# Sub-layer ends of a two-layer decoder trunk: three chunk pairs block by block, a written order for TensorE there, and the last output in quarters

## The chip, the core and the metric

The kernel runs on one NeuronCore of a Trainium2 chip. The metric is the device time of one execution in microseconds (us); the time of before is the median of three executions.

## What is computed

The reference is a two-layer decoder trunk on 256 tokens of width 1024, in fp32. Cut to what matters here:

```python
for l in range(2):
    ...                                   # modulation vectors sh, sc, g from c
    h = x * (1 + sc_a) + sh_a
    mixed = attention(h @ w_in[l])        # three head groups
    x = layer_norm(DN_ALPHA * x + (1 + g_a) * (mixed @ w_out[l]), ln_g[l, 0], ln_b[l, 0])
    h = x * (1 + sc_m) + sh_m
    f = jnp.square(jax.nn.relu(h @ mlp_w1[l])) @ mlp_w2[l]
    x = layer_norm(DN_ALPHA * x + (1 + g_m) * f, ln_g[l, 1], ln_b[l, 1])
```

So there are four sub-layer ends: a product with `w_out` or `mlp_w2`, a LayerNorm over the 1024 columns, and (but for the last) the modulated input of the next sub-layer, transposed.

## The kernel before

The 256 tokens are two blocks of 128 partitions. Every fp32 product is made of three fp32r products: each weight tile is split into a high part `whi` (ScalarE copies, L179) and a low part `wlo` (VectorE, or GpSimd where named, subtracts, L180), and so are the activations (`hT`, `mx`). The split weights go round ten buffers of 1024 columns (pool `spl`, tag "w"); the raw weights come by DMA from SyncE's queue (L138) into four buffers (`raw`).

`w_out` and `mlp_w2` are taken in chunks of 128 rows, two to a pair (one raw buffer): four pairs for `w_out` (`wo`, L1051 to L1053), sixteen for `mlp_w2` (`m2`, L1116 to L1118). A chunk's work for one block and one half of the 1024 columns is three matmuls of 512 columns (hi·hi, hi·lo, lo·hi); "products" below are such threes. Two accumulators of 512 columns per block collect them in PSUM. All pairs but the last two are done for both blocks as they come. The last two are the end: block 0 first, then block 1, so that block 0's normalization runs under block 1's products. `m1` (L368, L369, L371, L372, L1100 to L1103) makes one pair's input `FT` of `mlp_w2`: a product with `mlp_w1`, Relu, Square, and the split of the result.

`transition` is the end of three of the four sub-layers. For each block: times the gate and the residual, and statistics, on VectorE (`times` L405, `sums` L409, `spread` L412, `stats` L416 to L420, with a power on GpSimd); the scaled rows `P` on VectorE and ScalarE (L427, L425, L426); eight transposes on TensorE (`turn`, L454); scale and shift in PSUM (`modulate`, L463 on VectorE, L461 on ScalarE); the high part of `hT` on ScalarE (`high`, L466) and the low part on VectorE (`low`, L470). Behind that stands `work`, the first products of the next sub-layer, as rows (`v_tile`, L385: 24 matmuls named `mmv` for one block and 256 columns, in the order hT hi·w hi, hT lo·w hi, hT hi·w lo). After the `wo` end, `work` is three tiles for each block (`m1_rows`): `v_tile`, Relu and Square on ScalarE (L1083, L1084), and two transposes (`tp`<-`fr`, L1087), whose result is split (L1091, L1092). After layer 0's MLP it is one `v_tile` of 280 columns and two tiles with a copy (`kr`, L1001) and two transposes (L1004) each. `pool_split` gives a piece of the coming weights to GpSimd. `last_norm` is the end of the last sub-layer: it writes the output, block 0 in columns 0:640 and 640:1024 on GpSimd (L539), block 1 in halves on VectorE (L563, L566), and stores them from SyncE's queue (L535).

The order on each engine comes from a scheduler, except inside `manual_schedule`, where the engines named keep the order of the code: VectorE, ScalarE and GpSimd in `transition`, VectorE and GpSimd in `last_norm`. TensorE is not among them. Between the ends, `filler` puts steps of the modulation vectors' work (16 MB of weights over VectorE) into the loop over the MLP's pairs.

Of the kernel before, what the change touches and what calls it, by code (L numbers as in the profile page):

```python
# [120 lines left out]
def trunk_kernel(ctx: ExitStack, tc: tile.TileContext, a):  # L121
    nc = tc.nc
# [47 lines left out]

    SPARE = dict(P=4, qk=3, mx=4)

    def parts(t, n, eng=None, tag="w"):

        if tag == "w":
            hi, lo = (spl.tile([128, 1024], F32R, name=k, tag="w")[:, :n] for k in ("whi", "wlo"))
        else:
            hi, lo = (att.tile([128, 1024], F32R, name=k, tag=tag, bufs=SPARE[tag])[:, :n] for k in ("whi", "wlo"))
# [294 lines left out]
    def transition(products, accs, G, lnb, rnd, weights, spare, work):  # L473

        N = [Norm(b, accs[b], G, lnb) for b in range(2)]
        H = [MakeH(b, N[b], ROUND[rnd]) for b in range(2)]
# [3 lines left out]
        pool_split = lambda: weights and weights.pop(0)(nc.gpsimd)  # L480
        with tc.manual_schedule(engines={E.DVE, E.Activation, E.Pool}):
            for h in range(2):
                products(0, (h,))
                N[0].half(h)
            N[0].stats()
            pool_split()
            pool_split()
            N[0].scaled()
            for jj in range(2):
                H[0].turn(jj)  # L490
            products(1, (0, 1))
            H[0].modulate(0)
# [36 lines left out]
    def last_norm(products, accs, G, lnb):  # L529
# [4 lines left out]
        def store(n, c0, c1):  # L534
            nc.sync.dma_start(a["out"][0, n.b * 128:(n.b + 1) * 128, c0:c1], x[:, n.b, c0:c1])  # L535

        def on_pool(n, c0, c1):
            for i, op in enumerate((OP.mult, OP.add)):
                nc.gpsimd.tensor_tensor(x[:, n.b, c0:c1], (n.r[:, c0:c1], x[:, n.b, c0:c1])[i], lnb[:, i, c0:c1], op=op)  # L539
            store(n, c0, c1)  # L540

        with tc.manual_schedule(engines={E.DVE, E.Pool}):
            n = N[0]
            for h in range(2):
                products(0, (h,))
                n.half(h)
# [6 lines left out]
            n = N[1]  # L553
            for h in range(2):
                products(1, (h,))
                n.half(h)
            n.stats()
            on_pool(N[0], 640, D)
            cuts = ((0, 512), (512, D))
            for c0, c1 in cuts:  # L560
                s = slice(c0, c1)
                o = n.halves[c0 // 512]
                nc.vector.scalar_tensor_tensor(o, o, n.mv[:, 0:1], lnb[:, 0, s], op0=OP.subtract, op1=OP.mult)  # L563
            for c0, c1 in cuts:
                s = slice(c0, c1)
                nc.vector.scalar_tensor_tensor(x[:, 1, s], n.halves[c0 // 512], n.ve[:, 1:2], lnb[:, 1, s],  # L566
                                               op0=OP.mult, op1=OP.add)
                store(n, c0, c1)

# [353 lines left out]
    for l in range(DEPTH):  # L923
# [119 lines left out]

        def wo(b, c2, hs):
            for k, h in ((k, h) for k in range(2) for h in hs):
                c = 2 * c2 + k
                hi, lo = WO[c]
                mh, ml = MX[c2][:, 0, k, b * 128:(b + 1) * 128], MX[c2][:, 1, k, b * 128:(b + 1) * 128]
                s = slice(h * 512, h * 512 + 512)
                o = accs[b][h]  # L1050
                nc.tensor.matmul(o, mh, hi[:, s], start=c == 0, stop=False)  # L1051
                nc.tensor.matmul(o, mh, lo[:, s], start=False, stop=False)  # L1052
                nc.tensor.matmul(o, ml, hi[:, s], start=False, stop=c == 7)  # L1053

        for c2 in range(2):
            WO.extend(split(rawload(a["w_out"][l, c2]), 2, 1024))
            for b in range(2):
                wo(b, c2, (0, 1))
        for c2 in range(2, 4):
            WO.extend(split(rawload(a["w_out"][l, c2]), 2, 1024))  # L1060

# [43 lines left out]
        def load_w2(g):  # L1105
            W2[g] = split(rawload(a["mlp_w2"][l, g]), 2, 1024)

        def m2(g, b, hs):
            f = FT[g]
            t = slice(b * 128, (b + 1) * 128)  # L1110
            for i, h in ((i, h) for i in range(2) for h in hs):
                o = accs[b][h]
                s = slice(h * 512, h * 512 + 512)
                hi, lo = W2[g][i]
                first, lastk = g == 0 and i == 0, g == NG - 1 and i == 1
                nc.tensor.matmul(o, f[:, 0, i, t], hi[:, s], start=first, stop=False)  # L1116
                nc.tensor.matmul(o, f[:, 0, i, t], lo[:, s], start=False, stop=False)  # L1117
                nc.tensor.matmul(o, f[:, 1, i, t], hi[:, s], start=False, stop=lastk)  # L1118

        before = [p for g in range(EARLY) for p in w1_steps(g)]  # L1120
        end = transition(lambda b, h: [wo(b, c2, h) for c2 in (2, 3)], accs, ROUND[l, 3], lnb, (l, 2), before, SPARES[0],
                         [lambda b, g=g: m1_rows(g, b) for g in range(EARLY)])
# [4 lines left out]
        accs = [[ps.tile([128, 512], F32, name="m2", tag=t) for _ in range(2)] for t in ("acc", "sc")]  # L1127
        for g in range(NG - 2):
            with tc.issue_after(end[0]), tc.issue_after(end[1]):
                if EARLY <= g + 2 < NG:  # L1130
                    m1(g + 2)
                load_w2(g)
            for b in range(2):
                m2(g, b, (0, 1))
# [7 lines left out]
        tail = lambda b, h, m2=m2: [m2(g, b, h) for g in (NG - 2, NG - 1)]  # L1142
        if l < DEPTH - 1:
# [73 lines left out]
```

## Time and profile before

| | us |
|---|---|
| median of three runs (705.74 to 707.02) | 705.89 |
| the profiled execution, its own time | 706.43 |
| its span, first to last instruction | 704.7 |
| what lies around the span | 1.7 |
| TensorE busy in the span | 674.1 (96%) |
| VectorE busy | 492.3 (70%) |
| ScalarE busy | 402.6 (57%) |
| GpSimd busy | 39.1 (6%) |

Busy time is from the profiler's records of one execution; matmuls are pipelined and the end of one is modelled, so that spacing from start to start tells what a matmul costs. The mean granted TensorE clock was 0.991 of full speed.

### The profile page before, as it was taken

The numbers are of one execution on the slowest core, as the hardware profiler recorded it, in microseconds if no ns is written. First come the engines' busy times: TensorE is split into PE (matmuls) and PEld (weight loads), VectorE is DVE, ScalarE is ACT, GpSimd is POOL, SyncE is SP. The second block draws the span as 40 slices with busy tenths as digits, with TensorE's granted clock in tenths as the row PEclk, the third lists the DMA queues.
The fourth block names the chain that finished last, engine by engine and source line by source line (L and its number), as shares of the span: only waits on it lengthen the run. The fifth ranks groups of instructions, "written<-read, shape, count | busy, mean of one in ns | idle before, by whom it ended". The sixth has DMA issues, their size and how long they took to land.

```text
span 704.7 us, 11146 instructions
## 1 busy us (share of the span) xinstructions
PE 674.1 (96%) x4284; PEld 550.9 (78%) x4284; DVE 492.3 (70%) x947; ACT 402.6 (57%) x781; POOL 39.1 (6%) x39
## 2 busy tenths in 40 slices
PE   5998899999999999999998999999999999999994
PEld 4898658458788888888878977867788888888883
DVE  3455965657799879798977976657779855555556
ACT  2345473785665546656555447598474655656550
POOL 0000000000400000000013020000220000000003
PEclk9999999999999999999999999999999999999998
DMA  9998686568459989798873757710538955555501
GB/s 337 350 353 312 224 319 231 169 236 312 162 183 363 346 309 344 283 344 327 326 262 120 282 226 274 272 39 23 183 117 294 373 214 195 212 183 180 180 0 60
DMA packets 29553, 167.68 MB, mean 238 GB/s; under 512 B 3199, under 2 KB 6683, under 8 KB 11964
## 3 DMA queue, kind: packets, MB, share of 16 engines
q1 hardware_dynamic: 29436, 166.94, 65.0%
q8 instruction: 34, 0.56, 0.3%
q14 instruction: 19, 0.16, 0.1%
q0 software_dynamic: 64, 0.02, 0.0%
HBM read 165.87 MB, written 1.08 MB: 237 GB/s over the span
## 4 chain that ended last, share of the span: by engine, by line
PE 89%; DVE 4%; ACT 3%; issue 1%; POOL 1%; DMA 1%; SPq 0%; POOLq 0%; DVEq 0%
PE mm L368 14%; PE m L1116 8%; PE m L1117 8%; PE m L1118 8%; PE mmv L385 7%; PE mm L369 7%; PE s L680 3%; PE tp L648 3%; PE gv L168 3%; PE mm L355 2%; PE mm L357 2%; PE mm L356 2%; PE wo L1051 2%; PE wo L1053 2%; PE acc L696 2%; PE wo L1052 2%
## 5 line engine op out<-in xcount | busy, mean ns | idle before, releaser
L180 DVE TENSOR_TENSOR wlo<-raw,whi 128x1024 fp32r<-128x1024 f32 (+2 forms) x166 | 196.8, 1203 | 56.5 <-ACT whi L179 54.9
L179 ACT ACTIVATE whi<-raw 128x1024 fp32r<-128x1024 f32 (+2 forms) x175 | 179.2, 1041 | 56.8 <-PE wo L1052 17.2
L368 PE MATMUL mm<-hT,whi 128*128 128x512 f32 x416 | 148.3, 398 | 0.0
L369 PE MATMUL mm<-hT,wlo 128*128 128x256 f32 x416 | 117.0, 281 | 0.9 <-DVE wlo L180 0.9
L1116 PE MATMUL m<-whi,mx 128*128 128x512 f32 x256 | 100.1, 391 | 0.0
L1117 PE MATMUL m<-wlo,mx 128*128 128x512 f32 x256 | 100.0, 391 | 0.0
L1118 PE MATMUL m<-whi,mx 128*128 128x512 f32 x256 | 99.5, 390 | 0.0
L368 PEld LDWEIGHTS mm<-hT,whi 128*128 128x128 f32 x416 | 78.2, 188 | 20.3 <-ACT whi L179 0.8
L369 PEld LDWEIGHTS mm<-hT,wlo 128*128 128x128 f32 x416 | 78.5, 189 | 2.5 <-DVE wlo L180 1.6
L234 DVE SCALAR_TENSOR_TENSOR qk<-raw,se,qk 128x1024 f32<-128x1024 f32 x56 | 71.4, 1286 | 2.5 <-DMA raw<-in_ada_dram 1.9
L371 ACT ACTIVATE P<-mm 128x256 f32<-128x256 f32 x52 | 19.7, 378 | 73.0 <-PE mm L369 73.0
L385 PE MATMUL mmv<-whi,hT 128*128 128x256 f32 (+2 forms) x352 | 55.9, 304 | 4.7 <-ACT hT L466 4.7
L1116 PEld LDWEIGHTS m<-whi,mx 128*128 128x128 f32 x256 | 48.1, 188 | 11.2 <-ACT whi L179 0.8
L1118 PEld LDWEIGHTS m<-whi,mx 128*128 128x128 f32 x256 | 48.1, 188 | 10.1
L1117 PEld LDWEIGHTS m<-wlo,mx 128*128 128x128 f32 x256 | 48.0, 188 | 8.9
L385 PEld LDWEIGHTS mmv<-whi,hT 128*128 128x128 f32 x352 | 48.8, 194 | 6.9 <-ACT hT L466 5.9
L636 ACT ACTIVATE P<-P,sxt 128x128 f32<-128x128 f32 (+1 forms) x96 | 42.6, 446 | 17.2 <-DVE sxt L634 17.0
L355 PE MATMUL mm<-hT,whi 128*128 128x256 f32 x128 | 37.4, 292 | 0.0
L357 PE MATMUL mm<-hT,wlo 128*128 128x256 f32 x128 | 37.0, 289 | 0.0
L356 PE MATMUL mm<-hT,whi 128*128 128x256 f32 x128 | 36.8, 287 | 0.0
L634 DVE CUSTOM_DVE_ANT_0 P<-s,bias 128x128 f32<-128x128 f32 (+1 forms) x80 | 25.7, 351 | 14.4 <-PE s L680 12.0
L1103 DVE TENSOR_TENSOR mx<-P,mx 128x512 fp32r<-128x512 f32 x26 | 17.9, 690 | 25.6 <-ACT mx L1102 25.6
(215 smaller groups left out, 1090.4 us busy)
## 6 DMA issues: line engine op xcount, KB each, us to landing
raw<-in_mlp_w_dram SPq DMA_DIRECT2D x64, 1024.0 KB, 6.5
raw<-in_ada_dram SPq DMA_DIRECT2D x32, 1024.0 KB, 5.9
raw<-in_adag_dram SPq DMA_DIRECT2D x16, 1024.0 KB, 6.7
raw<-in_w_in_dram SPq DMA_DIRECT2D x9, 1024.0 KB, 6.1
raw<-in_cmp_w_dram SPq DMA_DIRECT2D x8, 1024.0 KB, 6.8
raw<-in_w_out_dram SPq DMA_DIRECT2D x8, 1024.0 KB, 6.8
w<-in_w_in_dram SPq DMA_DIRECT2D x8, 396.0 KB, 7.2
w<-in_w_in_dram SPq DMA_DIRECT2D x8, 384.0 KB, 6.1
```

Of the source, the lines that this page charges most:

```text
L179: nc.scalar.activation(hi, t, AF.Copy)
L180: (eng or nc.vector).tensor_tensor(lo, t, hi.bitcast(F32), op=OP.subtract)
L234: nc.vector.scalar_tensor_tensor(ac, src, by, ac, op0=OP.mult, op1=OP.add)
L355: nc.tensor.matmul(o[:, i], hi[:, c], hT[:, 0, kc], start=kc == 0, stop=False, skip_group_check=True)
L356: nc.tensor.matmul(o[:, i], hi[:, c], hT[:, 1, kc], start=False, stop=False, skip_group_check=True)
L357: nc.tensor.matmul(o[:, i], lo[:, c], hT[:, 0, kc], start=False, stop=kc == KC - 1, skip_group_check=True)
L368: nc.tensor.matmul(o, hi[:, c], hT[:, :, kc], start=kc == 0, stop=False, skip_group_check=True)
L369: nc.tensor.matmul(o[:, 0], lo[:, c], hT[:, 0, kc], start=False, stop=kc == KC - 1, skip_group_check=True)
L385: nc.tensor.matmul(o, hT[:, x_, kc, t], ws[kc][w_], start=kc == 0 and x_ + w_ == 0, stop=kc == KC - 1 and w_ == 1)
L1116: nc.tensor.matmul(o, f[:, 0, i, t], hi[:, s], start=first, stop=False)
L1117: nc.tensor.matmul(o, f[:, 0, i, t], lo[:, s], start=False, stop=False)
L1118: nc.tensor.matmul(o, f[:, 1, i, t], hi[:, s], start=False, stop=lastk)
```

## The change

Each sub-layer end now takes three pairs block by block instead of two, and the code hands `transition` a list of products. TensorE is added to the engines that keep the order of the code, in `transition` and in `last_norm`, where ScalarE is added too. Block 0's eight transposes stand after seven of block 1's twelve products (`TURN`). Of the three pairs, one is split in pieces of 512 columns into buffers of their own (tag "u2"). In `transition`, `scaled` stands before the first `pool_split`, and the second tile of `work` before block 1's transposes. The last `m1` stands ahead of the end. The loop over the MLP's pairs has one turn less, and two filler steps in two turns of three. In `last_norm` block 1's second half is made in two quarters of 256 columns, and its last 192 columns are finished on ScalarE and GpSimd; block 0's output goes in halves.

```diff
+TURN = 6
...
-    SPARE = dict(P=4, qk=3, mx=4)
+    SPARE = dict(P=4, qk=3, mx=4, u2=11)
...
+            m = 512 if tag == "u2" else 1024
+            hi, lo = (att.tile([128, m], F32R, name=k, tag=tag, bufs=SPARE[tag])[:, :n] for k in ("whi", "wlo"))
...
+    def wide(t, small=False):
+
+        hs = [slice(0, 512), slice(512, 1024)]
+        if small:
+            return [[parts(t[:, i * 1024 + h * 512:i * 1024 + h * 512 + 512], 512, None, "u2") for h in range(2)]
+                    for i in range(2)]
+        return [[(hi[:, s], lo[:, s]) for s in hs] for hi, lo in split(t, 2, 1024)]
...
-        with tc.manual_schedule(engines={E.DVE, E.Activation, E.Pool}):
+        with tc.manual_schedule(engines={E.PE, E.DVE, E.Activation, E.Pool}):
             for h in range(2):
-                products(0, (h,))
+                for p in products(0, (h,)):
+                    p()
                 N[0].half(h)
             N[0].stats()
+            N[0].scaled()
             pool_split()
-            pool_split()
-            N[0].scaled()
-            for jj in range(2):
-                H[0].turn(jj)
-            products(1, (0, 1))
+            for i, p in enumerate(products(1, (0, 1))):
+                p()
+                if i == TURN:
+                    for jj in range(2):
+                        H[0].turn(jj)
...
             N[1].scaled()
+            late.append(work[1](0))
             for jj in range(2):
                 H[1].turn(jj)
-            late.append(work[1](0))
...
-        with tc.manual_schedule(engines={E.DVE, E.Pool}):
+        with tc.manual_schedule(engines={E.PE, E.DVE, E.Activation, E.Pool}):
...
-            on_pool(n, 0, 640)
...
-            on_pool(N[0], 640, D)
...
+                on_pool(n, h * 512, h * 512 + 512)
+            for p in products(1, (0,)):
+                p()
+            m.times(0)
+            m.sums(0)
+            for i in range(2):
+                nc.vector.bn_stats(m.st[:, i], m.halves[0][:, i * 256:i * 256 + 256])
+            for i in (2, 3):
+                for p in products(1, (1,), i % 2 * 256, 256):
+                    p()
+                quarter(m, i)
...
+            nc.scalar.activation(r, c, AF.Identity, bias=m.ve[:, 3:4])
+            nc.gpsimd.tensor_tensor(r, r, lnb[:, 0, 832:], op=OP.mult)
+            nc.scalar.activation(r, r, AF.Copy, scale=m.ve[:, 1:2])
+            nc.gpsimd.tensor_tensor(x[:, 1, 832:], r, lnb[:, 1, 832:], op=OP.add)
+            cuts = ((0, 512, m.halves[0]), (512, 832, m.halves[1][:, :320]))
...
+        for c2 in range(1, 4):
+            WO += wide(rawload(a["w_out"][l, c2]), c2 == 1)
...
-        for g in range(NG - 2):
+        for g in range(NG - 3):
...
-                filler(1 + g % 2)
+                filler(1 + (g % 3 > 0))
         filler(100)
-        for g in (NG - 2, NG - 1):
+        m1(NG - 1)
+        for g in (NG - 3, NG - 2, NG - 1):
             load_w2(g)
```

`quarter(m, i)` is `times`, `sums` and statistics on 256 columns. Three places show how the rows on an engine move; the numbers behind names are the tiles'.

TensorE at layer 0's `wo` end, where the first tile of `work` ends and its transposes stand. Before:

```order
L385 MATMUL mmv_1990<-wlo_1870,hT_89 128x256 x4
L385 MATMUL mmv_2036<-whi_1915,hT_89 128x256 x2
L385 MATMUL mmv_2036<-whi_1873,hT_89 128x256 x4
L385 MATMUL mmv_2036<-whi_1915,hT_89 128x256 x2
L1087 MATMUL tp_2018<-p1_78,fr_2015 128x128 x2
L385 MATMUL mmv_2036<-whi_1915,hT_89 128x256 x2
L385 MATMUL mmv_2036<-wlo_1874,hT_89 128x256 x4
```

Now:

```order
L395 MATMUL mmv_1994<-wlo_1850,hT_89 128x256 x4
L395 MATMUL mmv_1994<-wlo_1854,hT_89 128x256 x4
L1117 MATMUL tp_2022<-p1_78,fr_2019 128x128 x2
L395 MATMUL mmv_2034<-whi_1857,hT_89 128x256 x4
L395 MATMUL mmv_2034<-whi_1915,hT_89 128x256 x4
```

Before, eight matmuls of the second tile stand between a tile's last matmul and its transposes; now none does. The same holds at each tile of `work` there but the last, and in layer 1.

TensorE at layer 1's MLP end, from the last row of the last `m1` on (`mx` with a number is a pair's `FT`, `m2` an accumulator). Before, where this `m1` makes `mx_6590`:

```order
L369 MATMUL mm2_6611<-hT_89,wlo_6587 128x256
L1116 MATMUL m2_5451<-whi_6636,mx_6414 128x512
L1117 MATMUL m2_5451<-wlo_6637,mx_6414 128x512
L1118 MATMUL m2_5451<-whi_6636,mx_6414 128x512
L1116 MATMUL m2_5452<-whi_6636,mx_6414 128x512
L1117 MATMUL m2_5452<-wlo_6637,mx_6414 128x512
```

Now, where it makes `mx_6614`:

```order
L379 MATMUL mm2_6635<-hT_89,wlo_6611 128x256
L1147 MATMUL m2_5475<-whi_6660,mx_6438 128x512
L1148 MATMUL m2_5475<-wlo_6661,mx_6438 128x512
L1149 MATMUL m2_5475<-whi_6660,mx_6438 128x512
L1147 MATMUL m2_5475<-whi_6668,mx_6438 128x512
L1148 MATMUL m2_5475<-wlo_6669,mx_6438 128x512
L1149 MATMUL m2_5475<-whi_6668,mx_6438 128x512
L1147 MATMUL m2_5475<-whi_6678,mx_6526 128x512
```

Before, 24 matmuls with `mx_6414` (four accumulators) and six with another `FT` stand ahead of the first that reads `mx_6590`; now six with `mx_6438` and six with `mx_6526`, all on one accumulator, stand ahead of the first that reads `mx_6614`. Layer 0's MLP end moves in the same way.

VectorE at the end of the program, block 1's second half and the output (`st`, `mv` and `ve` are statistics, `lnb` the norm's gain and bias). Before:

```order
L405 TENSOR_TENSOR m2_5454<-m2_5454,G_5786 128x512
L409 SCALAR_TENSOR_TENSOR m2_5454<-x_101,m2_5454 128x512
L412 BN_STATS st_6689<-m2_5454 128x6
L416 BN_AGGR mv_6765<-st_6689 128x2
L418 TENSOR_SCALAR ve_6767<-mv_6765 128x1
L419 TENSOR_SCALAR ve_6767<-mv_6765 128x1
L563 SCALAR_TENSOR_TENSOR m2_5453<-m2_5453,mv_6765,lnb_5448 128x512
L563 SCALAR_TENSOR_TENSOR m2_5454<-m2_5454,mv_6765,lnb_5448 128x512
L566 SCALAR_TENSOR_TENSOR x_101<-m2_5453,ve_6767,lnb_5448 128x512
L566 SCALAR_TENSOR_TENSOR x_101<-m2_5454,ve_6767,lnb_5448 128x512
```

Now, from the fourth quarter on (the same three rows, for the third quarter, stand just ahead):

```order
L554 TENSOR_TENSOR m2_5478<-m2_5478,G_5722 128x256
L555 SCALAR_TENSOR_TENSOR m2_5478<-x_101,m2_5478 128x256
L556 BN_STATS st4_6698<-m2_5478 128x6
L426 BN_AGGR mv_6823<-st4_6698 128x2
L428 TENSOR_SCALAR ve_6825<-mv_6823 128x1
L429 TENSOR_SCALAR ve_6825<-mv_6823 128x1
L596 SCALAR_TENSOR_TENSOR m2_5477<-m2_5477,mv_6823,lnb_5472 128x512
L596 SCALAR_TENSOR_TENSOR m2_5478<-m2_5478,mv_6823,lnb_5472 128x320
L598 SCALAR_TENSOR_TENSOR x_101<-m2_5477,ve_6825,lnb_5472 128x512
L598 SCALAR_TENSOR_TENSOR x_101<-m2_5478,ve_6825,lnb_5472 128x320
```

The three operations behind the last matmul have shrunk from 512 to 256 columns, and the last pair's second operation from 512 to 320. Both quarters lie in one accumulator, `m2_5478`, and in the built program the first matmul of the last quarter waits for L556 of the quarter before it.

## Rows read from the trace of the kernel before

**Rows 1.** Page, part 1: busy time of each engine, share of the span, instructions.

```profile
PE 674.1 (96%) x4284; PEld 550.9 (78%) x4284; DVE 492.3 (70%) x947; ACT 402.6 (57%) x781; POOL 39.1 (6%) x39
```

**Rows 2.** Waits of TensorE by releaser: us in all, number, longest.

```profile
PE mmv L385 <- ACT hT L466: 4.7, 3, 2.2
```

**Rows 3.** Two windows: length; PE, PEld, DVE, ACT, POOL busy; clock; DMA share; GB/s.

```profile
204.00:360.00 156.00, 155.54 (x794) 129.07 (x793) 132.09 (x146) 90.44 (x130) 0.00 (x0) 1.00 0.88 323
375.00:376.00 1.00, 1.00 (x7) 1.00 (x6) 1.00 (x2) 0.00 (x0) 1.00 (x1) 0.50 0.00 0
```

**Rows 4.** Timeline of TensorE at layer 0's `wo` end: start, length, instructions, [idle<-releaser].

```profile
179.72 0.66 PE L454 MATMUL tp<-p,P 128*128 128x128 f32 x4 [0.38 <-DVE P L427]
180.13 0.47 PE L1053 MATMUL wo<-whi,mx 128*128 128x512 f32 x1
...
183.70 2.89 PE L385 MATMUL mmv<-whi,hT 128*128 128x256 f32 x22 [1.26 <-ACT hT L466]
...
187.38 1.12 PE L385 MATMUL mmv<-whi,hT 128*128 128x256 f32 x8
188.47 0.44 PE L1087 MATMUL tp<-p,fr 128*128 128x128 f32 x2
...
196.34 0.40 PE L1087 MATMUL tp<-p,fr 128*128 128x128 f32 x2
```

**Rows 5.** The same stretch on ScalarE.

```profile
187.59 0.38 ACT L1083 ACTIVATE fr<-mmv 128x256 f32<-128x256 f32 x1 [2.51 <-PE mmv L385]
188.00 0.42 ACT L1084 ACTIVATE fr<-fr 128x256 f32<-128x256 f32 x1
...
191.36 1.82 ACT L461 ACTIVATE tp<-tp,sb 128x128 f32<-128x128 f32 x4 [0.20 <-PE tp L454]
...
194.85 1.10 ACT L179 ACTIVATE whi<-raw 128x1024 fp32r<-128x1024 f32 x1
```

**Rows 6.** The same stretch on VectorE.

```profile
182.10 0.69 DVE L405 TENSOR_TENSOR wo<-wo,G 128x512 f32<-128x512 f32 x1
...
184.88 0.68 DVE L470 TENSOR_TENSOR hT<-tp,hT 128x512 fp32r<-128x512 f32 x1
```

**Rows 7.** Timeline of TensorE at layer 0's MLP end.

```profile
373.00 4.05 PE L385 MATMUL mmv<-whi,hT 128*128 128x280 f32 x21 [2.19 <-ACT hT L466]
376.85 1.61 PE L385 MATMUL mmv<-wlo,hT 128*128 128x280 f32 x8
378.29 1.48 PE L385 MATMUL mmv<-whi,hT 128*128 128x256 f32 x11
...
387.13 1.19 PE L385 MATMUL mmv<-wlo,hT 128*128 128x280 f32 x8
388.16 2.06 PE L385 MATMUL mmv<-whi,hT 128*128 128x256 f32 x16
```

**Rows 8.** Timeline from the last `m1` on: its last matmul and the split of its result.

```profile
678.17 0.28 PE L369 MATMUL mm<-hT,wlo 128*128 128x256 f32 x1
...
679.34 0.36 ACT L371 ACTIVATE P<-mm 128x256 f32<-128x256 f32 x1
...
680.61 0.41 DVE L372 TENSOR_TENSOR P<-P,mm 128x256 f32<-128x256 f32 x1
...
681.05 0.63 ACT L1100 ACTIVATE P<-P 128x512 f32<-128x512 f32 x1 [1.35 <-DVE P L372]
...
683.05 0.69 DVE L1103 TENSOR_TENSOR mx<-P,mx 128x512 fp32r<-128x512 f32 x1 [2.02 <-ACT mx L1102]
```

**Rows 9.** Timeline of the program's end: last matmul, VectorE behind it.

```profile
694.40 0.39 PE L1118 MATMUL m<-whi,mx 128*128 128x512 f32 x1
...
694.83 0.70 DVE L405 TENSOR_TENSOR m<-m,G 128x512 f32<-128x512 f32 x1 [0.56 <-PE m L1118]
...
698.72 1.40 DVE L566 SCALAR_TENSOR_TENSOR x<-m,ve,lnb 128x512 f32<-128x512 f32 x2
```

More of the change, by code (lines that the diff above doesn't have):

```diff
@@ L535, in store, with quarter @@
             nc.sync.dma_start(a["out"][0, n.b * 128:(n.b + 1) * 128, c0:c1], x[:, n.b, c0:c1])
+        def quarter(n, i):
+            s = slice(i * 256, i * 256 + 256)
+            h, t = n.halves[i // 2], slice(i % 2 * 256, i % 2 * 256 + 256)
+            nc.vector.tensor_tensor(h[:, t], h[:, t], n.G[:, s], op=OP.mult)
+            nc.vector.scalar_tensor_tensor(h[:, t], x[:, n.b, s], RT2, h[:, t], op0=OP.mult, op1=OP.add)
+            nc.vector.bn_stats(n.st[:, i], h[:, t])
         def on_pool(n, c0, c1):
@@ L540, in on_pool @@
             store(n, c0, c1)
-        with tc.manual_schedule(engines={E.DVE, E.Pool}):
-            n = N[0]
+        n, m = N
+        m.st = sm.tile([128, 4, 6], F32, name="st4", bufs=1)
+        with tc.manual_schedule(engines={E.PE, E.DVE, E.Activation, E.Pool}):
             for h in range(2):
-                products(0, (h,))
+                for p in products(0, (h,)):
+                    p()
                 n.half(h)
@@ L1042, in trunk_kernel, with wo @@
         WO = []
[L1044 to L1060, printed above, removed]
+        def wo(b, c, h):
+            c2, k = divmod(c, 2)
+            hi, lo = WO[c][h]
+            mh, ml = MX[c2][:, 0, k, b * 128:(b + 1) * 128], MX[c2][:, 1, k, b * 128:(b + 1) * 128]
+            o = accs[b][h]
+            nc.tensor.matmul(o, mh, hi, start=c == 0, stop=False)
+            nc.tensor.matmul(o, mh, lo, start=False, stop=False)
+            nc.tensor.matmul(o, ml, hi, start=False, stop=c == 7)
+        WO += wide(rawload(a["w_out"][l, 0]))
+        for b in range(2):
+            for c, h in ((c, h) for c in range(2) for h in range(2)):
+                wo(b, c, h)
+        for c2 in range(1, 4):
+            WO += wide(rawload(a["w_out"][l, c2]), c2 == 1)
         NG = FF // 256
@@ L1105, in load_w2, with m2 @@
         def load_w2(g):
-            W2[g] = split(rawload(a["mlp_w2"][l, g]), 2, 1024)
-        def m2(g, b, hs):
+            W2[g] = wide(rawload(a["mlp_w2"][l, g]), g == NG - 3)
+        def m2(g, i, b, h, c0=0, n=512, l=l):
             f = FT[g]
             t = slice(b * 128, (b + 1) * 128)
[L1111 to L1118, printed above, removed]
+            s = slice(c0, c0 + n)
+            o = accs[b][h][:, s]
+            hi, lo = (w[:, s] for w in W2[g][i][h])
+            first, lastk = g == 0 and i == 0, g == NG - 1 and i == 1
+            late = dict(skip_group_check=l == DEPTH - 1 and g > NG - 4)
+            lastk = lastk or l == DEPTH - 1 and g == NG - 4 and i == 1
+            nc.tensor.matmul(o, f[:, 0, i, t], hi, start=first, stop=False, **late)
+            nc.tensor.matmul(o, f[:, 0, i, t], lo, start=False, stop=False, **late)
+            nc.tensor.matmul(o, f[:, 1, i, t], hi, start=False, stop=lastk, **late)
         before = [p for g in range(EARLY) for p in w1_steps(g)]
-        end = transition(lambda b, h: [wo(b, c2, h) for c2 in (2, 3)], accs, ROUND[l, 3], lnb, (l, 2), before, SPARES[0],
+        end = transition(lambda b, hs: [lambda c=c, h=h: wo(b, c, h) for c in range(2, 8) for h in hs], accs,
+                         ROUND[l, 3], lnb, (l, 2), before, SPARES[0],
                          [lambda b, g=g: m1_rows(g, b) for g in range(EARLY)])
@@ L1133, in trunk_kernel @@
             for b in range(2):
-                m2(g, b, (0, 1))
+                for i, h in ((i, h) for i in range(2) for h in range(2)):
+                    m2(g, i, b, h)
             with tc.issue_after(end[1]):
```

29 lines of the change are left out of this document (12 added, 17 removed).

## Prediction, made before the changed kernel was run

> **What bounds the kernel now.** I read the busy times first: TensorE is busy for 674.1 of 704.7 us [rows 1], so the change can win only TensorE's idle time, its waste at half clock and the tail, and loses what it adds to these. The list of waits shows what stands at the sub-layer ends: three waits for the high part of `hT` on ScalarE, 4.7 in all [rows 2]. The reader is to see there the first matmul of the next sub-layer waiting at each end, 1.26 at layer 0's `wo` end (and about as long in layer 1) and 2.19 at layer 0's MLP end [rows 4, 7]. A smaller one, 0.38, is at the first transposes [rows 4]. Between the ends the window 204 to 360 shows TensorE idle for 156.00 - 155.54 = 0.46 [rows 3]: what is moved within that stretch can win nothing. At the end of the program nothing covers VectorE: from the last matmul's start at 694.40 it has six operations of 512 columns and some small ones, 694.83 to 700.12 [rows 9]. So I looked at each place where the change fixes TensorE's order, for what it must now wait for with nothing else to do.
>
> **The `wo` ends, twice.** *Removed:* the products of the third pair lie between block 0's statistics and its transposes (seven products of three), and five products, 15 matmuls, behind the transposes. A matmul of 512 columns takes (694.40 - 678.17 - 0.11)/71 = 0.227 [rows 8, 9], for 72 of them lie between those two starts, so 15 are 3.4. Before, seven matmuls of the products (1.6) stood among and behind the transposes from 179.72 on, and the wait of 1.26 came after them [rows 4]: 2.9 to cover. I take both waits as gone: 0.38 + 1.26 = -1.64.
>
> *Added, transposes of `work`:* each tile's two transposes read `fr`, which ScalarE makes from the whole tile by Relu (0.38) and Square (0.42) [rows 5]. In the row for 187.38 the first tile is over and eight matmuls of the second run; the transposes start at 188.47 [rows 4], 0.05 after Square's end at 188.42. So the eight matmuls exactly cover the chain, 188.47 - 187.38 = 1.09. In the new order nothing stands between tile and transposes for five of the six tiles, and the built program makes the transposes wait for that Square. Four such waits are 4.36. The third tile's wait is longer: its Relu stands on ScalarE behind block 1's shift and high part, and a weight split of 1.10 comes between Relu and Square [rows 5]. ScalarE's chain from 191.36 to the transposes at 196.34 [rows 4, 5] is 4.98; it begins 0.2 after block 1's transposes; TensorE has only that one tile meanwhile, 24 matmuls of (187.38 - 183.70)/30 = 0.123, 2.95 [rows 4]. So 4.98 + 0.2 - 2.95 = 2.2 (below: 1.09, were ScalarE free).
>
> *Added, the low part:* the first tile now keeps its own order, and its 13th matmul needs the second low part. That ended at 184.88 + 0.68 = 185.56, and 183.70 + 12 x 0.123 = 185.18 [rows 4, 6]: 0.4 late, and 1.1 if one operation of 0.69 more stands ahead on VectorE, as `times` does. I take 0.7 (0 to 1.1). Before, the scheduler had other matmuls there.
>
> One end: 4.36 + 2.2 + 0.7 - 1.64 = +5.6; two: **+11.2**. Queued behind each wait is the whole of TensorE; VectorE and ScalarE hold nothing that another engine could use in that time.
>
> **Layer 0's MLP end.** Removed: the wait of 2.19, and what followed it. In 375 to 376 the granted clock is 0.50 of full speed, the lower of the two levels (1.2 GHz), while it is 1.00 from 204 to 360 [rows 3]. The 29 matmuls of 280 columns from 373.00 to 378.29 took 5.29; eight of them at 387.13 took 1.03, 0.129 each [rows 7], so 29 at full clock are 3.74: 1.55 lost. Behind the waits of 1.26 the matmuls ran at 0.123, at once [rows 4]: no loss. Added: the low part, 0.7, and two of the `kr` tiles' transposes behind their copy, with one ScalarE operation where `work` has two: 1.09 - 0.42 = 0.67 each. -2.19 - 1.55 + 0.7 + 1.34 = **-1.7**.
>
> On this row the Trainium skill has a rule that speaks against the change ("TensorE: Matmul & The Clock Gate", section "HAM oscillation — how this bites in real kernels"): matmuls in bursts with waits between them let the clock fall, and each burst begins at the lower level. The trace agrees after the wait of 2.19 and not after that of 1.26. By the rule the 2.2 waits at both `wo` ends would cost as much again; that is the first rival.
>
> **The last `m1` directly ahead of the end.** Its `FT` passes Relu and a copy, three ScalarE steps and a subtraction: 0.36 + 0.41 + 3 x 0.63 + 0.69 = 3.35, with handovers 3.7 [rows 8]. As it ran, it took 678.28 to 683.74, 5.5, with weight splits in between. Before, 30 matmuls (6.8) covered it; now 12 (2.7) do. Wait: 3.7 - 2.7 = 1.0 in layer 1 where the split stands behind; in layer 0 a chunk of the next layer's weights is split on the same engines, 1.10 more [rows 5], 2.1. Sum **+3.1** (below 0.6, if the chain of layer 0 is as free and handovers are quicker; above 2.8 + 3.9 = 6.7, as it ran).
>
> **Weights of the third pair.** The third pair's split parts are needed 18 matmuls, 4.1, earlier than in a loop over both blocks. Four new splits of half width cost no more than the two they replace, and ScalarE is idle for 302.1 of 704.7 us [rows 1], but in layer 0 VectorE is busy 132.09 of 156 ahead of the end [rows 3]. I take **+0.7**, a third of two splits of 1.10 (0 to 2.2).
>
> **Filler steps.** As many in all, two turns of three with two. In the window VectorE has 24 us free and TensorE 0.46 idle [rows 3]: **0**, covered by the four raw buffers; if a turn overran, a split of 1.10 (0 to 2).
>
> **The tail.** The first 256-column matmul of the last quarter waits for three VectorE operations on the quarter before (same accumulator). An operation of 256 columns takes 0.41 [rows 8], so 3 x 0.41 with handovers is 1.35, plus some 0.3 for the last matmul to drain: +1.65. 36 matmuls of 0.123 in place of 18 of 0.227: 4.43 - 4.09 = +0.3. Behind the last matmul three operations shrink from 0.70 to 0.41, -0.9, and two of the last four from 512 to 320 columns of 0.70 x 320/512, -0.5 [rows 9]. The 192 columns on ScalarE and GpSimd (two of 0.36 and two of about 39.1/39 = 1.0 [rows 1]: 2.7) lie beside VectorE's 2.3 and may end 0.4 later. Sum: 1.65 + 0.3 - 1.4 = **+0.5** (-0.5 to 1).
>
> **Sum.** 11.2 - 1.7 + 3.1 + 0.7 + 0.5 = +13.8. The profiled execution took 706.43 (span 704.7 and 1.7 around it), 0.54 over the median of 705.89, so I take that off: 706.43 + 13.8 - 0.54 = **719.7**.
>
> **Rivals.**
> *The clock falls after the 2.2 waits.* For: the row at half clock after 2.19. Against: the wait comes after a tile at full speed and lies in a dense stretch. Price as there, 1.55 at each of two ends: 722.8.
>
> *TensorE is not held by the waiting transposes* (the other side). If matmuls behind them ran meanwhile, the waits of 13.1 (twice 4.36 + 2.2), the `kr` ones of 1.3 and the 3.1 for `FT` would vanish: 719.7 - 17.5 = 702.2. It decides from the point at which these 17.5 shrink by 13.8, to under a fifth. Against: at 179.72 TensorE waited 0.38 for the transposes' input and the `wo` matmul that stood behind came only at 180.13 [rows 4], though its own inputs were old.
> The Trainium skill says the same ("TensorE: Matmul & The Clock Gate", section "Step-by-step: what each phase is for"): only weight loads are pulled ahead, "The MATMULs themselves stay in program order". By it this rival gives nothing; the row agrees.
>
> *More waiting.* `FT` as it ran (+3.6) and two splits late (+1.5): 724.8. For: VectorE is at 85% ahead of layer 0's end. Against: in layer 1 it has no filler.
>
> *Less waiting.* The third tile 1.09 (-2.2), the low part in time at three ends (-2.1), `FT` 0.6 (-2.5), weights in time (-0.7): 712.2.
>
> *It changes nothing:* were the built order the same, 705.9; but the order shown above differs at each place.
>
> **How the numbers follow.** Forecast 0.56 with its own range 715.5 to 721.5 (half of each bound above); clock 0.18; more waiting 0.10; less waiting 0.09; other side 0.05; nothing 0.02. The predicted time is the forecast's, 719.7. The range 712 to 726 takes in all but the other side, no change and the outer halves of the two waiting rivals: about 0.84. A measurement of this kernel tells about 0.2% (1.4 us): faster 0.05, same 0.02, slower 0.93.
>
> **What would show it.** Right: among TensorE's waits eight for `fr` of about 1.1 and two of 2 or more; no 1.26 or 2.19 for `hT`, but waits of under a us for its low part; a wait for `mx` in each layer before the 13th matmul of an MLP end; one wait of 1.65 for VectorE ahead of the last 18 matmuls; full clock at layer 0's MLP end. TensorE's busy time stays at about 674. Wrong: transposes that start behind a tile without idle time, or idle time between 204 and 360 that the filler's new pace makes. I would be wrong most if ScalarE's chain overlapped the tile's own last matmuls, which no row here shows.

## The result, and the profile after

The changed kernel takes **724.68 us** (median of 4 runs, 722.83 to 726.17) against 705.83 (4 runs): ratio 1.0259, interval 1.0244 to 1.0273, 18.9 us slower. Forecast were 719.7, with 712 to 726. The profiled execution, 722.83 with a span of 721.1, is the quickest of the four, so 16.4 of the 18.9 can be read in its trace; the other 2.5 are the profiled executions' distances to their medians, +1.85 after and -0.60 before.

Part 1 of the page of after:

```profile
PE 677.2 (94%) x4302; PEld 550.3 (76%) x4302; DVE 491.7 (68%) x959; ACT 403.4 (56%) x791; POOL 39.9 (6%) x41
```

TensorE does the same work (3.1 busy us more, against [rows 1]) in a span 16.4 longer: the loss is waiting. TensorE's waits in after, by releaser (us in all, number, longest):

```profile
PE tp L1117 <- ACT fr L1114: 11.6, 10, 2.1
...
PE m L1147 <- ACT mx L1132: 1.9, 2, 1.4
...
PE m L1147 <- DVE st L556: 1.5, 1, 1.5
PE mmv L395 <- DVE hT L480: 1.3, 3, 0.5
PE wo L1082 <- DVE wlo L182: 1.3, 3, 0.8
PE tp L1036 <- ACT kr L1033: 1.1, 2, 0.6
PE sw L824 <- ACT ct L1051: 0.8, 1, 0.8
PE acc L805 <- ACT pT L682: 0.8, 1, 0.8
...
PE tp L680 <- DVE P L674: 0.5, 1, 0.5
```

None of these rows is in the list of before. The 4.7 for the high part of `hT` [rows 2] is gone, and ten waits of the transposes for `fr` stand in its place. TensorE at layer 0's `wo` end, where [rows 4] showed no wait for `fr`:

```profile
182.98 1.60 PE L395 MATMUL mmv<-whi,hT 128*128 128x256 f32 x12
185.04 0.74 PE L395 MATMUL mmv<-whi,hT 128*128 128x256 f32 x4 [0.46 <-DVE hT L480]
185.61 1.11 PE L395 MATMUL mmv<-wlo,hT 128*128 128x256 f32 x8
187.64 0.44 PE L1117 MATMUL tp<-p,fr 128*128 128x128 f32 x2 [0.92 <-ACT fr L1114]
187.84 2.15 PE L395 MATMUL mmv<-whi,hT 128*128 128x256 f32 x16
...
194.90 1.12 PE L395 MATMUL mmv<-wlo,hT 128*128 128x256 f32 x8
198.15 0.44 PE L1117 MATMUL tp<-p,fr 128*128 128x128 f32 x2 [2.13 <-ACT fr L1114]
```

One tile can be followed here: twelve matmuls, a wait for the second low part, the last twelve, and then TensorE stands until Square is done. ScalarE behind the third tile:

```profile
193.20 1.83 ACT L471 ACTIVATE tp<-tp,sb 128x128 f32<-128x128 f32 x4 [1.40 <-PE tp L464]
...
196.43 0.41 ACT L1113 ACTIVATE fr<-mmv 128x256 f32<-128x256 f32 x1
196.70 1.09 ACT L181 ACTIVATE whi<-raw 128x1024 fp32r<-128x1024 f32 x1
197.64 0.45 ACT L1114 ACTIVATE fr<-fr 128x256 f32<-128x256 f32 x1
```

The weight split of 1.09 stands between Relu and Square, as before the change [rows 5]. There the wait had other matmuls beside it; here all of TensorE waits for it.

**Where the 16.4 came from.** I lined up the two traces by the start of the k-th matmul of a group (`wo` or `m`) in a layer. An offset is after minus before; the last column is what was added since the row above.

| matmul | before | after | offset | added |
|---|---|---|---|---|
| layer 0, first `wo` | 156.04 | 156.31 | +0.27 | 0.27 (start of the program) |
| its 61st `wo` | 172.60 | 173.89 | +1.29 | 1.02 (late weights of the third pair) |
| its 49th `m` | 226.98 | 232.36 | +5.38 | 4.09 (`wo` end) |
| its 361st `m` | 364.07 | 371.52 | +7.45 | 2.07 (`FT` late) |
| layer 1, first `wo` | 475.79 | 483.69 | +7.90 | 0.45 (MLP end and attention) |
| its 37th `wo` | 495.49 | 505.95 | +10.46 | 2.56 (first products) |
| its 49th `m` | 555.34 | 569.80 | +14.46 | 4.00 (`wo` end) |
| its 361st `m` | 689.19 | 704.68 | +15.49 | 1.03 (`FT` late) |
| its last `m` | 694.40 | 711.94 | +17.54 | 2.05 (quarters) |
| end of the span | 704.7 | 721.1 | +16.4 | -1.14 (behind the last matmul) |

The last two rows' places in the trace of after, TensorE and then VectorE:

```profile
708.07 0.28 PE L1149 MATMUL m<-whi,mx 128*128 128x256 f32 x1
709.81 0.39 PE L1147 MATMUL m<-whi,mx 128*128 128x256 f32 x1 [1.46 <-DVE st L556]
...
709.32 0.43 DVE L556 BATCH_NORM_STATS2 st<-m 128x6 f32<-128x256 f32 x1
712.26 0.43 DVE L554 TENSOR_TENSOR m<-m,G 128x256 f32<-128x256 f32 x1 [2.50 <-PE m L1149]
...
715.20 1.20 DVE L598 SCALAR_TENSOR_TENSOR x<-m,ve,lnb 128x512 f32<-128x512 f32 x2
```

The two quarters, which should overlap, run one after the other: TensorE waits 1.46 for VectorE, then VectorE 2.50 for TensorE. Against [rows 9] the part behind the last matmul is shorter by the 1.14 of the table.

### The profile page after: what moved, and what is told of

Its sections match the earlier page's. It is cut to its first block, busy times and chain, and to the rows that moved or that the text cites. A ratio compares the mean times of both kernels' runs of the same rounds, so it can differ in the third digit from the quotient of the medians.

```text
span 721.1 us, 11205 instructions
## 1 busy us (share of the span) xinstructions
PE 677.2 (94%) x4302; PEld 550.3 (76%) x4302; DVE 491.7 (68%) x959; ACT 403.4 (56%) x791; POOL 39.9 (6%) x41
## 3 DMA queue, kind: packets, MB, share of 16 engines
HBM read 165.87 MB, written 1.08 MB: 232 GB/s over the span
## 4 chain that ended last, share of the span: by engine, by line
PE 81%; ACT 7%; DVE 7%; DMA 2%; issue 2%; POOL 0%; SPq 0%; POOLq 0%; DVEq 0%; ACTq 0%
PE mm L378 13%; PE m L1147 8%; PE m L1149 8%; PE m L1148 8%; PE mm L379 7%; PE mmv L395 6%; PE s L712 3%; PE gv L169 3%; PE tp L680 2%; DVE wlo L182 2%; PE acc L728 2%; ACT whi L181 2%; PE mm L341 2%; PE wo L1082 2%; PE wo L1081 2%
## 5 line engine op out<-in xcount | busy, mean ns | idle before, releaser
L182 DVE TENSOR_TENSOR wlo<-raw,whi 128x1024 fp32r<-128x1024 f32 (+3 forms) x174 | 196.9, 1155 | 52.9 <-ACT whi L181 51.7
L181 ACT ACTIVATE whi<-raw 128x1024 fp32r<-128x1024 f32 (+3 forms) x183 | 178.5, 1002 | 53.7 <-PE mm L378 17.3
L1147 PE MATMUL m<-whi,mx 128*128 128x512 f32 (+1 forms) x262 | 101.7, 388 | 3.3 <-ACT mx L1132 1.9
L1148 PE MATMUL m<-wlo,mx 128*128 128x512 f32 (+1 forms) x262 | 101.0, 386 | 0.0
L1149 PE MATMUL m<-whi,mx 128*128 128x512 f32 (+1 forms) x262 | 100.8, 386 | 0.0
L1147 PEld LDWEIGHTS m<-whi,mx 128*128 128x128 f32 x262 | 49.2, 188 | 14.8 <-ACT mx L1132 2.7
L1149 PEld LDWEIGHTS m<-whi,mx 128*128 128x128 f32 x262 | 49.2, 188 | 10.8 <-DVE mx L1133 0.9
L395 PE MATMUL mmv<-whi,hT 128*128 128x256 f32 (+2 forms) x352 | 53.0, 299 | 1.3 <-DVE hT L480 1.3
L395 PEld LDWEIGHTS mmv<-whi,hT 128*128 128x128 f32 x352 | 47.3, 189 | 2.6 <-DVE hT L480 1.9
```

The source lines that it names most:

```text
L395: nc.tensor.matmul(o, hT[:, x_, kc, t], ws[kc][w_], start=kc == 0 and x_ + w_ == 0, stop=kc == KC - 1 and w_ == 1)
L1147: nc.tensor.matmul(o, f[:, 0, i, t], hi, start=first, stop=False, **late)
L1148: nc.tensor.matmul(o, f[:, 0, i, t], lo, start=False, stop=False, **late)
L1149: nc.tensor.matmul(o, f[:, 1, i, t], hi, start=False, stop=lastk, **late)
```

## The experiments

In each, the time beside it of before is 705.92 to 706.21 on the same chip. The offsets quoted are against the trace of before, at the matmuls of the table.

**1. TensorE's order free again in the three ends.**

```diff
-        with tc.manual_schedule(engines={E.PE, E.DVE, E.Activation, E.Pool}):
+        with tc.manual_schedule(engines={E.DVE, E.Activation, E.Pool}):
             for h in range(2):
```

> The changed kernel, but TensorE's order is left to the scheduler again in the three ends before the last (three pairs, the buffers, the last m1's place and the end of the output as changed). Theory 'order': the waits of TensorE behind the transposes of fr (11.6 us in the trace of after), of kr (1.1) and for the low part of hT (1.3) go, and of the old 4.7 for the high part some 2 come back: 724.7 - 12 = 713 (709 to 716). Rival 'third pair' (what costs is the third pair itself: late weights, less to do under the attention): 720 or more, with fr's waits gone and others in their place.

702.87, ratio 0.9963 (0.9951 to 0.9976): 21.8 less than the changed kernel, and faster than before. No wait for `fr`, `kr` or the low part is left. The same place of its trace:

```profile
181.71 3.02 PE L395 MATMUL mmv<-whi,hT 128*128 128x256 f32 x23
184.56 1.12 PE L395 MATMUL mmv<-wlo,hT 128*128 128x256 f32 x8
185.52 1.12 PE L395 MATMUL mmv<-whi,hT 128*128 128x256 f32 x8
186.61 0.44 PE L1117 MATMUL tp<-p,fr 128*128 128x128 f32 x2
```

The 23 are the first tile's and some of the second's mixed, which hides the low part, and eight of the second's stand ahead of the transposes. TensorE's written order in the three ends alone turned a change worth -3.0 into one of +18.9. It went beyond the 709 to 716 expected: no wait for the high part of `hT` came back, for which I had allowed 2; the stretch from layer 0's MLP end (361st `m`) to layer 1's first `wo` gained 4.2 (-3.73 in place of +0.45); late weights, `FT` in layer 0 and layer 1's first products cost 1.0, 1.4 and 1.3 less; and the 1.85 between the changed kernel's median and its trace went too.

**2. The order written out, but the transposes behind the next tile.** `m1_rows` and `rows` return their transposes as a function, called one tile later:

```diff
             late.append(work[1](0))
+            late[0] = late[0] and late[0]()
             for jj in range(2):
                 H[1].turn(jj)
+            late[1] = late[1] and late[1]()
...
-            late = [w(1) for w in work]
-            for f in late:
+            turn = work[2](0)
+            for w in work:
+                t = w(1)
+                f = turn and turn()
                 if f:
                     f()
+                turn = t
+            turn()()
```

> The changed kernel with TensorE's order still written out, but each tile's two transposes behind the next tile's 24 matmuls (2.95 us, against a chain of 1.1 and once 5.0 on ScalarE). Theory 'order, and there the place of the transposes': fr's ten waits fall from 11.6 to under 2, kr's to 0, the others stay: 724.7 - 10.5 = 714 (711 to 717). Rival 'a fixed order is dear wherever the rows stand': other waits take their place, 720 or more.

707.43, ratio 1.0026 (1.0015 to 1.0037): 17.3 less. TensorE in its trace at the same place:

```profile
185.71 1.12 PE L395 MATMUL mmv<-wlo,hT 128*128 128x256 f32 x8
186.66 2.06 PE L395 MATMUL mmv<-whi,hT 128*128 128x256 f32 x16
188.56 1.10 PE L395 MATMUL mmv<-wlo,hT 128*128 128x256 f32 x8
189.50 0.38 PE L1125 MATMUL tp<-p,fr 128*128 128x128 f32 x2
189.72 1.09 PE L464 MATMUL tp<-p,P 128*128 128x128 f32 x8
```

A tile of 24 now covers the chain, and no transposes wait for `fr` or `kr`. The `wo` ends fall from +4.09 and +4.00 to -1.84 and -1.86: 5.9 at each, and `fr`'s waits were 11.6 in all. So a fixed order isn't dear wherever the rows stand; the rival falls. It is still 4.6 slower than the free order of experiment 1: by the offsets, 2.0 of this is `FT` in layer 0, 1.0 late weights and 1.3 layer 1's first products. The 17.3 exceed the 10.5 that I expected by three things: the two `wo` ends gave 11.8, where I had under 10; the stretch from layer 0's MLP end to layer 1's first `wo` goes from +0.45 to -3.59, 4.04 where I had 1.1 for `kr`; and the changed kernel's median lies 1.85 over its profiled execution while this one's lies 0.07 over.

**3. Two pairs, with the order written out.** The last `m1` is in the loop with that, as before the change, and no pair goes to the buffers of 512 columns.

```diff
-TURN = 6
+TURN = 3
...
-        for c2 in range(1, 4):
-            WO += wide(rawload(a["w_out"][l, c2]), c2 == 1)
+        for c2 in range(2, 4):
+            WO += wide(rawload(a["w_out"][l, c2]))
...
-        for g in range(NG - 3):
+        for g in range(NG - 2):
...
-        m1(NG - 1)
-        for g in (NG - 3, NG - 2, NG - 1):
+        for g in (NG - 2, NG - 1):
             load_w2(g)
```

> The changed kernel with two pairs done block by block instead of three (as before the change), TensorE's order still written out, no buffers of 512 columns, and block 0's transposes after four of block 1's eight products; the last m1 is then in the loop again. Theory 'order': fr's waits stay at about 11.6; gone are the waits for FT (1.0 and 2.1 by the offsets), for late w_out weights (1.3) and what the attention of layer 1 lost for want of other matmuls (about 2), while the high part of hT may come later by 0.5 at each end: 724.7 - 5.5 = 719 (716 to 722). Rival 'third pair': back to 708 or less.

721.76, ratio 1.0233 (1.0219 to 1.0248), as the theory 'order' has it and 13.8 over the rival's 708. `fr` waits 11.6 again. The offsets say what the third pair and the place of the last `m1` cost together under a written order: from the first `wo` to its 61st 0.00 (was 1.02), at layer 1's first products 0.00 (was 2.56), from the 49th to the 361st `m` +0.11 and 0.00 (were 2.07 and 1.03). In return the transposes of `P` wait three times, 4.5 in all, and the quarters' wait is 2.2. The two `wo` ends add 5.83 and 7.25. They have the same waits of 2.12 for `fr` on the third tile, but the clock fell behind the second of them (at 533.43) and not behind the first (at 198.17):

```profile
197.00:200.00 3.00, 1.83 (x16) 1.83 (x17) 3.00 (x6) 1.50 (x3) 0.00 (x0) 1.00 0.00 0
...
533.00:536.00 3.00, 2.57 (x15) 2.57 (x16) 3.00 (x4) 0.76 (x3) 0.00 (x0) 0.71 0.00 0
```

The rows are windows of 3 us: length; PE, PEld, DVE, ACT, POOL busy; clock; DMA share; GB/s.

**4. The last `m1` a turn earlier.**

```diff
                     m1(g + 2)
+                if g == NG - 4:
+                    m1(NG - 1)
...
         filler(100)
-        m1(NG - 1)
```

> The changed kernel with the last m1 a turn earlier, in the loop, ahead of that turn's 24 matmuls. If its FT was what the 13th matmul of each MLP end waited for, the two offsets of 2.1 (layer 0) and 1.0 (layer 1) go: 724.7 - 3.1 = 721.6 (720.5 to 723). Rival 'something else holds that matmul' (the weights' split, which stands beside it): no change.

719.20, ratio 1.0193 (1.0179 to 1.0207). The wait for `mx` is gone and the offsets added there are +0.26 and +0.02 in place of 2.07 and 1.03: the term of 3.1 was about right. The time fell by 5.5, not 3.1. The wait for `sw` (0.8) is gone as well, and part of the rest is the clock: three of its five executions (718.56 to 719.20) had a mean granted clock of 0.995 and two (721.15, 723.11) 0.990. Against the changed kernel's one execution at 0.994 (722.83) the three lie 3.6 to 4.3 lower, which is the 3.1 and the 0.8. The one that was profiled is the slowest, and shows where (windows as above):

```profile
195.00:198.00 3.00, 1.63 (x14) 1.43 (x12) 1.22 (x4) 2.97 (x8) 0.00 (x0) 1.00 0.25 104
198.00:201.00 3.00, 2.25 (x11) 2.25 (x12) 3.00 (x5) 1.08 (x3) 0.00 (x0) 0.66 0.00 0
201.00:204.00 3.00, 2.56 (x17) 2.35 (x15) 1.29 (x2) 1.44 (x2) 0.00 (x0) 0.77 0.00 0
```

In the profiled execution of after the same stretch, with the same waits, was at full clock:

```profile
196.00:199.00 3.00, 0.87 (x8) 0.85 (x8) 2.67 (x5) 2.47 (x7) 0.00 (x0) 1.00 0.00 0
199.00:202.00 3.00, 2.46 (x21) 2.26 (x19) 2.73 (x4) 1.54 (x4) 0.00 (x0) 1.00 0.00 0
```

**5. Block 1's second half in one piece.** The last 192 columns stay on ScalarE and GpSimd.

```diff
-            m.times(0)
-            m.sums(0)
-            for i in range(2):
-                nc.vector.bn_stats(m.st[:, i], m.halves[0][:, i * 256:i * 256 + 256])
-            for i in (2, 3):
-                for p in products(1, (1,), i % 2 * 256, 256):
-                    p()
-                quarter(m, i)
+            m.half(0)
+            for p in products(1, (1,)):
+                p()
+            m.half(1)
```

> The changed kernel with block 1's second half in one piece of 512 columns again (products, then times, sums and statistics); the last 192 columns stay on ScalarE and GpSimd. Theory 'the last quarter waits for its accumulator': the offset of 2.05 that the quarters cost ahead of the last matmul goes, and about 0.9 of what they win behind it is given back: 724.7 - 1.1 = 723.6, with the wait of 1.5 for st gone. Rival 'the quarters pay': 725 or more. The spread of this kernel's times (3 us) is as large as the difference, so the last stretch of the trace decides.

722.24, ratio 1.0228 (1.0211 to 1.0245). Between the 361st and the last `m` nothing is added in place of 2.05, and behind the last matmul -0.25 in place of -1.14: the quarters lose 1.2. Here too the profiled execution (724.70) had the clock low behind the third tile's wait at both `wo` ends, which added 5.53 each in it, against 4.09 and 4.00 in after. The first of them:

```profile
196.00:199.00 3.00, 0.87 (x8) 0.67 (x7) 2.01 (x5) 2.76 (x7) 0.00 (x0) 1.00 0.00 0
199.00:202.00 3.00, 3.00 (x17) 3.00 (x17) 2.54 (x3) 0.75 (x2) 0.00 (x0) 0.57 0.00 0
202.00:205.00 3.00, 2.08 (x15) 1.88 (x14) 1.75 (x2) 1.49 (x3) 0.00 (x0) 0.87 0.00 0
```

**6. Free order, last `m1` earlier, one piece at the end** (the edits of 1, 4 and 5).

> Three edits of the changed kernel together: TensorE's order left to the scheduler in the three ends before the last, the last m1 a turn earlier, block 1's second half in one piece. If the terms add: 702.9 - 0.8 - 1.0 (the offsets at FT that the kernel with the free order still has in layers 0 and 1) - 1.1 (the quarters) = 700.0 (699 to 701.5), with no wait for mx or st left. Rival 'the scheduler gives it back elsewhere': 702 or more.

**701.22, ratio 0.9927 (0.9914 to 0.9941)**, the best of all: 4.7 faster than before. No wait for `mx` or `st` is left. It lacks 1.2 of the expected sum; its profiled execution reached the first `wo` 0.8 later than that of experiment 1 (156.70 against 155.89), ahead of everything that was edited.

**7. The transposes behind the next tile, two pairs at the `w_out` ends alone** (the edits of 2, and those of 3 on `w_out`).

```diff
-            for i, p in enumerate(products(1, (0, 1))):
-                p()
-                if i == TURN:
+            ps1 = products(1, (0, 1))
+            for i, p in enumerate(ps1):
+                p()
+                if i == {12: 6, 8: 3}[len(ps1)]:
```

> The kernel with the transposes behind the next tile, TensorE's order written out, and at the two w_out ends two pairs block by block instead of three (the MLP ends keep three). Theory 'a third w_out pair costs its late weights and the work that filled layer 1's attention': the offsets of about 1.1 at layer 0's w_out and 2.3 at layer 1's go; with fewer products to lie between, the transposes of P wait some 1.5 at each of the two ends again: 707.4 - 3.4 + 3.0 = 707.0 (705.5 to 708.5), the shares shown by the offsets. Rival 'the attention's loss has another cause': the offset of 2.3 at layer 1's w_out stays, 708.5 or more.

707.66, ratio 1.0023 (1.0014 to 1.0032). The additions of 1.02 and 2.56 are both gone (-0.01 and -0.02), so both belong to the third `w_out` pair; the transposes of `P` wait twice, 3.0 in all. The net is nothing, as worked out. The 2.56 has two parts. One is work that no longer lies under the attention: before the change 25 `wo` matmuls start between layer 1's first and the last matmuls of its attention (475.79 to 492.65), as in this kernel, and in after 17 (483.69 to 500.00). The other is a wait of 0.85 for late `wlo`, at the 29th. The free order tells them apart: experiments 1 and 6 have the same 17 and no such wait, and +1.27 and +1.31 there, with 0.00 for the late weights of layer 0. So about 1.3 comes with the third pair whatever the order on TensorE, and the written order adds 1.3 in layer 1 and 1.0 in layer 0, where it stands and waits for late weights.

**8. As 6, with two pairs at the `w_out` ends.**

> The kernel with the free order, the last m1 a turn earlier and one piece at the end, and two pairs block by block at the w_out ends. If the scheduler covers the waits with the next matmuls, the third w_out pair brings only its costs (0.9 late weights in layer 0, 1.3 in layer 1's attention): 700.0 - 1.5 = 698.5. Rival 'the third pair covers the w_out ends': the waits of 0.4 and 1.3 of before come back at each, 700 + 1.1 = 701.

703.12, ratio 0.9959 (0.9945 to 0.9973): my theory fell, and the rival is nearer, though its 701 was 2.1 too low. With a free order the third `w_out` pair is worth 1.9. The waits for the high part come back (1.6) and for `P` (0.9); the `wo` ends add +0.1 each, where those of experiment 6 add -1.75 and -1.50.

**9. Only the third tile's transposes behind the next tile** (`now` calls what a tile returns at once).

```diff
-            for w in work[2:]:
-                f = w(0)
-                if f:
-                    f()
-            late = [w(1) for w in work]
+            turn = work[2](0)
+            t = work[0](1)
+            turn()()
+            late = [now(t)] + [now(w(1)) for w in work[1:]]
```

> The changed kernel, but at each w_out end the third tile's transposes alone stand behind the next tile (in the MLP end nothing of weight moves: there it is the second kr tile). Each loses a wait of 2.1; eight waits of 0.92 stay. Theory 'the long wait lets the clock fall in some executions' (in the run with the last m1 in the loop the clock was 0.66 to 0.81 right behind that wait, and the changed kernel's times spread over 3.3 us): 724.7 - 2 x 2.2 - about 1.8 = 718.5, and the times agree within 1.5. Rival 'it is the sum of the waits that lets it fall': 720.3, with a spread of 3 as before.

719.24, ratio 1.0185 (1.0171 to 1.0199). Four of five executions lie within 0.7 (718.94 to 719.61) at a clock of 0.994. The fifth, 721.60 at 0.991, is the profiled one; its clock is 1.00 at both `wo` ends and falls to 0.84 and 0.73 from 500 to 508 instead, behind two waits of 1.2 for the split of layer 1's `w_out` weights (`whi`, then `wlo`). Each `wo` end gains 1.4 and not 2.1 (+2.69 and +2.62), because the low part of block 1, that the long wait had covered, now waits itself (2.8 in all, was 1.3). The theory asked for times within 1.5. Four executions keep to it and the fifth, 2.7 above the quickest, doesn't, and it fell behind shorter waits than 2.1: the theory isn't shown, and the rival isn't excluded.

**10. As 2, with the edits of 4 and 5.**

> TensorE's order written out, the transposes behind the next tile, the last m1 a turn earlier, block 1's second half in one piece. The terms add to 707.4 - 2.0 - 1.0 (FT) - 1.1 (quarters) = 703.3 (702 to 704.5), faster than before by 0.3%. If what was left of the loss lay elsewhere than in these places: 705 or more. Against the free order with the same edits (701.2) it should still lack the late low parts (2.0) and the work under layer 1's attention.

703.50, ratio 0.9959 (0.9947 to 0.9972), 0.2 from the sum. The places named account for the loss. Against experiment 6 it lacks 2.3, but not where I expected it. The low parts still wait 2.0 in its list, and yet its `wo` ends are not behind (-1.82 and -1.87, there -1.75 and -1.50), and from layer 0's MLP end to layer 1's first `wo` it lacks only 0.25. The 2.3 are the late weights: 1.02 more at layer 0's `w_out` and 1.24 more at layer 1's first products (+2.55 against +1.31).

## Why the prediction was right, and where its terms were not

The sign, the range and the mechanism held: the written order makes TensorE wait for the engine that it has just fed, at the transposes above all. The signs that it named came: ten waits for `fr`, two of them over 2, none for the high part, waits for `mx` and for `st`, and full clock at layer 0's MLP end. But the time lies above the inner range of 715.5 to 721.5, at the price of the rival "more waiting" (724.8), and not by that rival's cause: `FT` came out as forecast. By its own steps:

- **Transposes of `work`.** Forecast 6.56 for each end, and right. The list's idle times (four of 0.92, one of 2.13: 5.8) begin at the modelled end of a tile's last matmul. From start to start, as I had counted it, the first transposes come at 187.64, 1.20 behind the start of their tile's last matmul, where a next matmul would come 0.12 behind it: 1.08, and so 2.29 for the third tile, 6.6 in all.
- **The low part** 0.62 from start to start at each `wo` end (0.46 in the list; forecast 0.7).
- **The waits removed.** Here the `wo` end failed: I took them from the idle times, 0.38 + 1.26 = 1.64, and set them against added waits that I had counted from start to start. These are TensorE's rows of before ahead of the two waits of [rows 4]:

```profile
178.95 0.39 PE L1052 MATMUL wo<-wlo,mx 128*128 128x512 f32 x1
...
182.04 0.40 PE L1053 MATMUL wo<-whi,mx 128*128 128x512 f32 x1
```

With 0.23 for a matmul, the waits were 179.72 - 178.95 - 0.23 = 0.54 and 183.70 - 182.04 - 0.23 = 1.43, together 1.97. A wait of 0.46 for a `wlo` right behind each end, 0.62 from start to start, went as well, and so did three delays of 0.13 ahead of the transposes for `fr` of before; I had counted neither. An end came out at 4.0 to 4.1, not 5.6.
- **`FT`.** Forecast 2.1 and 1.0; 2.07 and 1.03.
- **Weights of the third pair.** Forecast 0.7; 1.02, but at layer 0's `w_out` and not at its MLP, and once more in layer 1 (below). That four splits of half width cost no more than two was wrong: four of 0.62 on ScalarE and of 0.69 on VectorE in after, against two of 1.05 and 1.22.
- **Layer 0's MLP end.** Forecast -1.7, measured +0.45. The gain was right: once the transposes lie behind the next tile the stretch gives -3.59, about the 2.19 and 1.55 that I had taken as removed. (Of the 29 matmuls that I read as 280 columns wide, five have 256; that moves the 1.55 by 0.04.) The price of the `kr` transposes was right too: 0.63 + 0.76 = 1.39 from start to start, forecast 1.34. What failed is that I put nothing behind them. Counted at equal work, after falls 4.05 behind experiment 2 in this stretch: 1.4 at `kr`, 0.5 more by 404 us, 0.7 at the wait for `sw`, 0.7 at a wait of the attention's transposes for their `P` at 443, and 0.7 ahead of it, for which I can name no row.
- **Layer 1's first products.** Not in my sum at all: +2.56. I had looked for what stands behind each waiting row, and not at what a longer end takes away from the stretch ahead of it (1.3) nor at weights that come late there (1.3). That was the main omission.
- **The tail.** Forecast +1.65 + 0.3 - 1.4 = +0.5; 2.05 - 1.14 = +0.9.
- **The clock.** In the trace of after it did not fall at the ends, and the sum needed nothing for it. In other executions it did: behind the same waits, the ends with a fall cost 1.4 to 1.5 more each in experiments 4 and 5, and the one in experiment 3 cost 1.4 more than that kernel's other end, against the 1.55 of this rival. The four executions of after are ordered by their mean granted clock: 722.83 at 0.994, 723.88 at 0.991, 725.48 at 0.989, 726.17 at 0.987. Beyond one at 60 us that every trace has, in the profiled executions 0.994 goes with no fall (after), 0.992 with one (experiment 3), 0.990 with two (experiment 4) and 0.987 with three (experiment 5, the third at 80 us), so an estimate from these is that after's had none, one, two and three. By this estimate the 1.85 by which the median lies above the profiled execution is the clock, and this rival came true in part of the executions. What the Trainium skill says of bursts and waits ("TensorE: Matmul & The Clock Gate", section "HAM oscillation — how this bites in real kernels") agrees with the traces of experiments 3 to 5 (0.57 to 0.87 behind such a wait) and not with that of after (1.00). The waits in the page's own case are longer than these, so the prediction asked more of that rule than the page states.
- **TensorE is not held by waiting transposes** fell: it did nothing while they waited, ten times.

The errors partly cancelled: 13.8 against 16.4, with 3.1 too much at the `wo` ends, 2.15 too little at the MLP end and 2.56 not seen, and 1.0 in smaller ones. That the sum came within 2.6 is luck as much as reading. It stays open what decides in which execution the clock falls.

## What to carry to other kernels

A written order must hold the producer's chain as well as its rows: where an engine's result goes through another engine and back, put at least that chain's length of other work between, which is what the scheduler had done and one tile's shift restored (17 us). Ask also what comes late elsewhere in the pinned stretch: late weights cost 1.0 and 1.3 us under the written order and nothing under the free one (experiments 2 and 1). Count added and removed waits in the same measure, from start to start. And free the order before judging the rest of such a change: the third `w_out` pair was worth 1.9 under a free order and nothing under a written one (experiments 7 and 8).

## What the runs showed of the hardware

The same program with the same waits of 2.12, in one execution, ran on at 1.00 of full clock behind one of them and at 0.71 and 0.72 in the 6 us behind the other (experiment 3); the two ends are 1.4 us apart. The same rows ran at 1.00 at both places in the profiled execution of after and at 0.57 to 0.87 at both in those of experiments 4 and 5. Such kernels spread (3.3, and 2.7 to 4.6 in experiments 3 to 5, against 1.3 to 2.2 in the six without that wait, 1, 2, 6 to 8 and 10), and this was the first sign of it, ahead of any row. It is no proof by itself: before, without these waits, also spread by 3.7 over 17 executions on one chip, through one at 708.86.
